# Loading each filler unit's weights one unit sooner in the attention stages of a hybrid attention block

## The chip, the cores and the metric

The kernel runs on one core of a Trainium2 chip. The metric is the device time of one execution, in microseconds (us); lower is better. The engines are named as in the profile: PE is TensorE (matmul), PEld its weight loads, DVE is VectorE, ACT is ScalarE, POOL is GpSimd, and SP is SyncE, whose queue issues most of the DMA transfers.

## The reference

One layer of a streaming encoder, for 1024 positions of 1024 channels, in float32: two attention branches side by side, merged by gates, and a feed-forward part.

```python
h = rms_norm(x, norm_mix[layer])
proj = h @ w_in[layer]
(sb_q, sb_k, sb_v, g_q, g_k, g_v, g_out, g_low, gate_sb, gate_gla) = jnp.split(
    proj, split_points, axis=-1)

o_sb = stick_breaking_attention(split_heads(sb_q, SB_HEADS).astype(f32),
                                split_heads(sb_k, SB_HEADS).astype(f32),
                                split_heads(sb_v, SB_HEADS).astype(f32))
...
o_gla = gla_chunked(split_heads(g_q, GLA_HEADS).astype(f32),
                    split_heads(g_k, GLA_HEADS).astype(f32),
                    split_heads(g_v, GLA_HEADS).astype(f32),
                    split_heads(log_a, GLA_HEADS))
...
mix = (jax.nn.sigmoid(gate_sb) * (o_sb @ w_proj_sb[layer])
       + jax.nn.sigmoid(gate_gla) * (o_gla @ w_proj_gla[layer]))
x = x + mix @ w_out[layer]

h2 = rms_norm(x, norm_mlp[layer])
x = x + jnp.square(jax.nn.relu(h2 @ w_ff1[layer])) @ w_ff2[layer]
return rms_norm(x, norm_final)
```

The stick-breaking attention has 8 heads of 64 channels. For each query it takes the sigmoids of the scores (`beta`) and of their negatives (`fail`), runs a product of the `fail` values over the keys from the nearest back, and weighs the values by `beta` times that product.

## The kernel before

**Products in three parts.** Every float32 operand is split into a high part `hi` (a cast on ACT) and a low part `lo` (a subtraction on DVE), and `mm3` forms hi·hi + hi·lo + lo·hi: three matmuls (lines 115 to 117) for each block of 128 channels.

**Stages.** First the RMSNorm, then the gated linear attention (GLA) of 4 heads, whose result goes to DRAM as `o_gla`, then the stick-breaking attention in four pairs of heads (`sb_core`, p = 0 to 3), then the projection of its result (`pa`), `w_out`, and the feed-forward part. An attention pair has 8 steps (`sb_step`); a step makes scores on PE (`pz`), sigmoids on ACT (`beta`, `fail`, lines 582 and 583), masks on POOL, a running product (line 589, "scan") and a multiplication on DVE, transposes on PE (`ptw`), a split into `w_hi` and `w_lo`, the products with the values (`poa`), and an addition into `o_sb` (line 619).

**Fillers.** Between the steps, `fill(n)` runs n entries of the list `fillers`, projections that don't depend on the step at hand. An entry is half of a unit. A unit has one weight tile of 128x8x128 (512 KB) and two products, one for each half of the positions. `load_cols` (through `load_w`) loads the tile into a buffer `raw` and splits it into `whi` and `wlo`. The pool gives `raw` two buffers (`bufs=2`), and `whi` and `wlo` two each. `queue_gate` units make the gates (`mmt`, then a copy and a store to DRAM). `queue_b` units make `o_gla @ w_proj_gla` (`pb`, line 669), multiply by the sigmoid of a gate (line 673: this also frees the bank of `pb`) and store the result. Fillers accumulate in the two banks of `ps_fill`.

**The last pair.** For p = 3 the list holds the rest of the earlier fillers, the last two gate units with their halves interleaved, and then the 8 `queue_b` units, two and two: first halves of units 0 and 1, then their second halves, and so on. The first `queue_b` entry of each half calls `load_b(half)`: four transfers of o_gla pieces of 512 KB (line 658), each into a `raw` buffer of the same two, each split into a part of `bt_hi` and `bt_lo`. Half 0 and half 1 have tiles of their own.

**What sets the order.** The program is not run in the order in which it is written. A scheduler decides at build time, engine by engine, in which order the instructions stand; each engine, and SP's queue, then takes its instructions strictly in that order, and waits for semaphores where data or a buffer is not ready. Buffers of one tag go round in the order of their allocation in the program.

Of the kernel before, what the change touches and what calls it, by code (L numbers as in the profile page):

```python
# [47 lines left out]
def hybrid_block_kernel(ctx, tc, x, norm_mix, w_in, w_gate_up, b_gate_up, gla_norm, w_proj_sb, w_proj_gla,  # L48
# [114 lines left out]
    stage = ctx.enter_context(tc.tile_pool(name="stage", bufs=2))  # L163

    fillers = []

    def fill(n=1):
        for _ in range(min(n, len(fillers))):
            fillers.pop(0)()

    def queue_unit(load, halves):
        w = []

        def half_unit(i):
            if not w:
                w.append(load())
            halves(w[0], i)

        for i in range(2):
            fillers.append(lambda i=i: half_unit(i))  # L180

    def queue_gate(c0, dst):
        def halves(w, half):
            acc = proj_t(w, half)
            raw = stage.tile([P, HALF], F32, tag="gate", name="gate", bufs=2)
            nc.scalar.copy(out=raw, in_=acc)
            nc.sync.dma_start(out=dst[:, half * HALF:(half + 1) * HALF], in_=raw)

        queue_unit(lambda: load_cols(w_in, c0), halves)
# [97 lines left out]
    def queue_gla_qk(h):  # L287
        res = [[None, None], [None, None]]

        def q_half(w, half):  # L290
            q1 = gw.tile([P, 4, 192], F32, tag="q1", name="q1", bufs=2)
            acc = proj_t(w, half)
            nc.scalar.mul(out=q1[:, :, 64:192], in_=acc.rearrange("p (c t) -> p c t", t=P), mul=float(P) ** -0.5)
            res[half][0] = q1

        def k_half(w, half):
            kT = gw.tile([P, 4, P], F32, tag="kT", name="kT", bufs=2)
            acc = proj_t(w, half)
            nc.scalar.copy(out=flat(kT), in_=acc)
            res[half][1] = kT  # L300

        n = len(fillers)
        queue_unit(lambda: load_cols(w_in, GQ + h * P), q_half)
        queue_unit(lambda: load_cols(w_in, GK + h * P), k_half)
        fillers[n:n + 4] = [fillers[n + i] for i in (0, 2, 1, 3)]
        return res
# [154 lines left out]
    qk = queue_gla_qk(0)  # L461
    vgs = [gla_vg(c, vo) for c in range(VG_START)]
    fill(2)
    for half in range(2):
        sl = slice(half * HALF, (half + 1) * HALF)
# [11 lines left out]

    pre = gla_pre(0, 0, *qk[0])
    fill(2)
    n_gate = 0  # L480
    n_vg = VG_START
    for h in range(G_HEADS):
        nxt = None
        if h + 1 < G_HEADS:
            nxt = queue_gla_qk(h + 1)
        while len(fillers) < sum(GLA_FILL):
            queue_gate(*gates[n_gate])
            n_gate += 1
        pre1 = None
        for c in range(NT):  # L490
            gla_core(h, c, pre if c < 4 else pre1, vgs.pop(0))
            while n_vg < min(h * NT + c + 1 + VG_AHEAD, G_HEADS * NT):
                if n_vg % NT == 0:
                    vo = [load_vo(n_vg // NT, j) for j in range(4)]
                vgs.append(gla_vg(n_vg % NT, vo))
                n_vg += 1
            fill(GLA_FILL[c])
            if c == 1:
                pre1 = gla_pre(h, 1, *qk[1])
            if c == 5 and nxt:  # L500
                pre_n = gla_pre(h + 1, 0, *nxt[0])
        if nxt:
            qk, pre = nxt, pre_n
# [684 lines left out]
```

## Time and profile before

| | us |
|---|---|
| median of 3 runs | 1673.47 |
| lowest and highest run | 1673.26 and 1673.96 |
| the profiled execution, its own time | 1675.34 |
| span of the profile, first to last instruction | 1673.6 |
| PE busy in the span | 1644.1 (98%) |

The mean granted clock of PE was 0.996 of full speed. Times in the trace count from the span's start. The profiled execution is a single one, so a sum made from its rows is compared with its own time first.

### The profile page before, as it was taken

What the parts mean: (1) busy time and instruction counts of PE and PEld (TensorE: products, weight loads), DVE (VectorE), ACT (ScalarE), POOL (GpSimd) and SP (SyncE); (2) the same over time, 40 slices, a digit from 0 to 9 for tenths busy, and PEclk for the clock granted to TensorE, in tenths of its full rate; (3) what the DMA queues carried; (4) which work ended last, traced back from release to release, by engine and by line L of the source; (5) the groups of instructions that cost most, each with busy time, mean ns of one, the idle gap of its engine ahead of it and who ended that gap; (6) DMA issues with size and microseconds to landing.
All of it is one profiled execution on the core that took longest, in us unless ns stands there. A gap on an engine that the chain in (4) does not pass through costs nothing.

```text
span 1673.6 us, 22678 instructions
## 1 busy us (share of the span) xinstructions
PE 1644.1 (98%) x8160; PEld 1377.9 (82%) x8160; DVE 1143.6 (68%) x1954; ACT 762.2 (46%) x1544; POOL 381.1 (23%) x376
## 2 busy tenths in 40 slices
PE   7999999999999999999999999999999999999997
PEld 5788888888888888888888788888888888888886
DVE  7677677665732768677876645887776764787795
ACT  6456455554532656565644422422222234444464
POOL 4001000000010021201110000598777640000161
PEclk9999999999999999999999999999999999999999
DMA  7103104022121121114426643454444467655453
GB/s 215 28 20 108 33 20 126 18 76 66 54 66 39 45 70 27 32 30 148 132 95 201 199 160 101 137 184 159 153 150 156 144 205 236 201 189 171 157 166 123
DMA packets 153952, 194.06 MB, mean 116 GB/s; under 512 B 11712, under 2 KB 91584, under 8 KB 153840
## 3 DMA queue, kind: packets, MB, share of 16 engines
q1 hardware_dynamic: 150464, 189.83, 35.6%
q10 hardware_dynamic: 3376, 2.79, 0.5%
q8 instruction: 64, 1.05, 0.3%
q14 instruction: 48, 0.39, 0.1%
HBM read 138.05 MB, written 54.53 MB: 115 GB/s over the span
## 4 chain that ended last, share of the span: by engine, by line
PE 87%; DMA 5%; DVE 4%; ACT 2%; issue 1%; POOL 1%; SPq 0%; ACTq 0%; POOLq 0%; DVEq 0%
PE mmt L115 7%; PE mmt L117 7%; PE mmt L116 7%; PE pp L115 6%; PE pp L116 6%; PE pp L117 6%; PE pq L117 6%; PE pq L115 6%; PE pq L116 6%; PE mmn L116 4%; PE mmn L117 4%; PE mmn L115 4%; PE sc L408 2%; PE pw L115 2%; PE pw L117 2%; PE pw L116 2%
## 5 line engine op out<-in xcount | busy, mean ns | idle before, releaser
L117 PE MATMUL mmt<-ht_hi,wlo 128*128 128x512 f32 x512 | 201.7, 394 | 2.7 <-DVE wlo L79 2.7
L115 PE MATMUL mmt<-ht_hi,whi 128*128 128x512 f32 x512 | 201.8, 394 | 1.3 <-DVE qs L543 1.3
L116 PE MATMUL mmt<-ht_lo,whi 128*128 128x512 f32 x512 | 201.3, 393 | 0.0
L108 POOL TENSOR_TENSOR rstd<-ms,mhalf 128x1 f32<-128x1 f32 x56 | 41.8, 749 | 648.1 <-DVE ms L104 420.2
L116 PE MATMUL pp<-wlo,whi 128*128 128x512 f32 x448 | 174.4, 389 | 0.0
L117 PE MATMUL pp<-whi,wlo 128*128 128x512 f32 x448 | 174.3, 389 | 0.0
L115 PE MATMUL pp<-whi 128*128 128x512 f32 x448 | 165.8, 389 | 0.0
L79 DVE TENSOR_TENSOR wlo<-raw,whi 128x1024 fp32r<-128x1024 f32 (+1 forms) x110 | 121.2, 1102 | 43.9 <-ACT whi L76 43.5
L76 ACT CAST whi<-raw 128x1024 fp32r<-128x1024 f32 (+1 forms) x112 | 95.8, 866 | 113.9 <-PE pq L116 34.9
L115 PE MATMUL mmn<-whi,ht_hi 128*128 128x512 f32 (+1 forms) x384 | 139.9, 365 | 0.4 <-DVE kl L558 0.4
L116 PE MATMUL mmn<-wlo,ht_hi 128*128 128x512 f32 (+1 forms) x384 | 139.2, 363 | 0.9 <-POOL wlo L79 0.9
L117 PE MATMUL mmn<-whi,ht_lo 128*128 128x512 f32 (+1 forms) x384 | 139.0, 362 | 0.0
L749 DVE TENSOR_TENSOR wlo<-raw,whi 128x512 fp32r<-128x512 f32 (+1 forms) x112 | 89.7, 801 | 68.2 <-ACT whi L1048 49.5
L115 PE MATMUL pq<-s_hi,whi 128*128 128x512 f32 x320 | 126.2, 395 | 0.0
L117 PE MATMUL pq<-s_hi,wlo 128*128 128x512 f32 x320 | 126.0, 394 | 0.0
L116 PE MATMUL pq<-s_lo,whi 128*128 128x512 f32 x320 | 125.6, 393 | 0.0
L1048 ACT CAST whi<-raw 128x512 fp32r<-128x512 f32 x96 | 59.7, 622 | 134.8 <-PE pp L117 68.2
L117 PEld LDWEIGHTS mmt<-ht_hi,wlo 128*128 128x128 f32 x512 | 96.3, 188 | 22.4 <-DVE wlo L79 3.8
L115 PEld LDWEIGHTS mmt<-ht_hi,whi 128*128 128x128 f32 x512 | 96.3, 188 | 19.9 <-issue 1.7
L116 PEld LDWEIGHTS mmt<-ht_lo,whi 128*128 128x128 f32 x512 | 96.4, 188 | 18.5
L115 PEld LDWEIGHTS pp<-whi 128*128 128x128 f32 x448 | 84.1, 188 | 17.6
L117 PEld LDWEIGHTS pp<-whi,wlo 128*128 128x128 f32 x448 | 84.1, 188 | 17.4
(295 smaller groups left out, 4019.0 us busy)
## 6 DMA issues: line engine op xcount, KB each, us to landing
raw<-in_w_in_dram SPq DMA_DIRECT2D x36, 512.0 KB, 4.0
raw<-in_w_ff_dram SPq DMA_DIRECT2D x36, 512.0 KB, 4.4
raw<-aop_S SPq DMA_DIRECT2D x64, 256.0 KB, 2.8
aop_A<-c SPq DMA_DIRECT2D x48, 256.0 KB, 3.2
aop_S<-s SPq DMA_DIRECT2D x48, 256.0 KB, 2.2
raw<-aop_A SPq DMA_DIRECT2D x48, 256.0 KB, 2.7
r<-in_w_ff_dram SPq DMA_DIRECT2D x48, 256.0 KB, 3.1
raw<-in_w_in_dram SPq DMA_DIRECT2D x32, 256.0 KB, 3.2
```

The source lines that it names most:

```text
L76: nc.scalar.copy(out=hi, in_=src)
L79: lo_eng.tensor_tensor(out=lo, in0=src, in1=hi.bitcast(F32), op=ALU.subtract)
L108: rstd_ins.append(nc.gpsimd.tensor_tensor(out=r, in0=ms, in1=mhalf, op=ALU.pow).ins)
L115: nc.tensor.matmul(ps, lhsT=sh, rhs=mh, start=first, stop=False)
L116: nc.tensor.matmul(ps, lhsT=sh, rhs=ml, start=False, stop=False)
L117: nc.tensor.matmul(ps, lhsT=sl, rhs=mh, start=False, stop=last)
L408: nc.tensor.matmul(sc[:P - H, i * 64:(i + 1) * 64], lhsT=lev[H][:, j, :P - H], rhs=right, start=True, stop=True)
L749: eng.tensor_tensor(out=out, in0=in0, in1=in1, op=ALU.subtract)
L1048: nc.scalar.copy(out=hi[:, 0], in_=raw[:, 0])
```

## The change

`queue_unit` registers each unit's load under its two entries (`get`, which does nothing once the tile is loaded). `fill`, before it runs an entry, calls the load of that entry and then the load of the entry that comes next. So in the program a unit's `raw`, `whi` and `wlo` tiles are allocated and its transfer issued one entry sooner, ahead of everything that the entry before allocates and issues. Nothing else is changed; the number of instructions of each kind is the same.

```diff
@@ -163,21 +163,31 @@
     stage = ctx.enter_context(tc.tile_pool(name="stage", bufs=2))
 
     fillers = []
+    loads = {}
 
     def fill(n=1):
         for _ in range(min(n, len(fillers))):
-            fillers.pop(0)()
+            f = fillers.pop(0)
+            if fillers and f in loads:
+                loads.pop(f)()
+            if fillers and fillers[0] in loads:
+                loads.pop(fillers[0])()
+            f()
 
     def queue_unit(load, halves):
         w = []
 
-        def half_unit(i):
+        def get():
             if not w:
                 w.append(load())
+
+        def half_unit(i):
+            get()
             halves(w[0], i)
 
         for i in range(2):
             fillers.append(lambda i=i: half_unit(i))
+            loads[fillers[-1]] = get
 
     def queue_gate(c0, dst):
         def halves(w, half):
```

The order of the instructions, as the scheduler left it, differs from before only in the last attention pair. In what follows, line numbers of the changed kernel are 10 higher than before (L668 is L658 of before, and so on).

**SP's queue, the loads of the last pair.** `raw<-in_w_in_dram` is the weight of a gate unit, `raw<-in_w_proj_gla_dram` that of a `queue_b` unit, `raw<-o_gla` a piece of `load_b`; `gate_a` is a store of a gate, `sg<-gate_b` a load of one. Before:

```order
L85 DMA raw<-in_w_in_dram 128x8x128
L85 DMA raw<-in_w_proj_gla_dram 128x8x128
L187 DMA gate_a<-gate 128x512
L658 DMA raw<-o_gla 128x2x512
L187 DMA gate_a<-gate 128x512 x2
L658 DMA raw<-o_gla 128x2x512 x2
L187 DMA gate_a<-gate 128x512
L658 DMA raw<-o_gla 128x2x512
L85 DMA raw<-in_w_proj_gla_dram 128x8x128
L667 DMA sg<-gate_b 128x512
L187 DMA gate_a<-gate 128x512
L658 DMA raw<-o_gla 128x2x512
```

Now:

```order
L85 DMA raw<-in_w_in_dram 128x8x128
L85 DMA raw<-in_w_proj_gla_dram 128x8x128
L197 DMA gate_a<-gate 128x512
L85 DMA raw<-in_w_proj_gla_dram 128x8x128
L197 DMA gate_a<-gate 128x512 x3
L668 DMA raw<-o_gla 128x2x512
L677 DMA sg<-gate_b 128x512
L197 DMA gate_a<-gate 128x512
L668 DMA raw<-o_gla 128x2x512
L677 DMA sg<-gate_b 128x512
L668 DMA raw<-o_gla 128x2x512 x6
```

The second weight of w_proj_gla stood behind the first four o_gla pieces; it now stands ahead of all eight, which follow in one sequence with no weight between them.

**ACT, where the second half of o_gla is cast.** `bt_hi_8561` is the tile of half 1 (L76 casts a piece of it), `beta` and `fail` are the sigmoids of an attention step. Before:

```order
L76 CAST bt_hi_8561<-raw 128x1024
L604 CAST w_hi<-ptw 128x256
L604 CAST w_hi<-ptw 128x128
L76 CAST bt_hi_8561<-raw 128x1024
L604 CAST w_hi<-ptw 128x128
L668 ACTIVATE sg<-sg 128x512
L582 ACTIVATE beta<-pz 128x512
L583 ACTIVATE fail<-pz 128x512
L582 ACTIVATE beta<-pz 128x384
L583 ACTIVATE fail<-pz 128x384
```

Now:

```order
L76 CAST bt_hi_8561<-raw 128x1024
L614 CAST w_hi<-ptw 128x128
L76 CAST bt_hi_8561<-raw 128x1024
L592 ACTIVATE beta<-pz 128x512
L593 ACTIVATE fail<-pz 128x512
L592 ACTIVATE beta<-pz 128x384
L593 ACTIVATE fail<-pz 128x384
L628 COPY o_sb_5041<-poa 64x256
L614 CAST w_hi<-ptw 128x256
L76 CAST bt_hi_8561<-raw 128x1024
```

The rows ahead of the first fence hold the casts of the first two pieces of half 1. So the four sigmoids stood behind the casts of all four pieces, and now stand behind those of the first two; the casts of the last two pieces moved behind them.

**DVE, at the same place.** `bt_lo_8562` is the low part of half 1, `sg<-pb` (L673, now L683) frees a bank of `pb`. Before:

```order
L79 TENSOR_TENSOR bt_lo_8562<-raw,bt_hi_8561 128x1024
L605 TENSOR_TENSOR w_lo<-ptw,w_hi 128x128
L673 TENSOR_TENSOR sg<-pb,sg 128x512
L589 SCALAR_TENSOR_TENSOR fail<-fail 128x895
L619 TENSOR_TENSOR o_sb_5041<-poa,o_sb_5041 64x256
L591 TENSOR_TENSOR beta<-beta,fail 128x895
L605 TENSOR_TENSOR w_lo<-ptw,w_hi 128x256
```

Now:

```order
L79 TENSOR_TENSOR bt_lo_8562<-raw,bt_hi_8561 128x1024
L615 TENSOR_TENSOR w_lo<-ptw,w_hi 128x128
L79 TENSOR_TENSOR bt_lo_8562<-raw,bt_hi_8561 128x1024
L599 SCALAR_TENSOR_TENSOR fail<-fail 128x895
L629 TENSOR_TENSOR o_sb_5041<-poa,o_sb_5041 64x256
L683 TENSOR_TENSOR sg<-pb,sg 128x512
L615 TENSOR_TENSOR w_lo<-ptw,w_hi 128x256
L601 TENSOR_TENSOR beta<-beta,fail 128x895
L79 TENSOR_TENSOR bt_lo_8562<-raw,bt_hi_8561 128x1024
```

The first release of a `pb` bank stood ahead of the scan of 895 elements; it now stands behind it and behind the addition into `o_sb`, and only the subtractions of the first two pieces of half 1 come ahead of the scan.

## Rows read from the trace of the kernel before

**Rows 1.** Page, parts 1 and 2: busy time and its tenths.
```profile
PE 1644.1 (98%) x8160; PEld 1377.9 (82%) x8160; DVE 1143.6 (68%) x1954; ACT 762.2 (46%) x1544; POOL 381.1 (23%) x376
PE   7999999999999999999999999999999999999997
```

**Rows 2.** Page, part 4: the chain that ended last.
```profile
PE 87%; DMA 5%; DVE 4%; ACT 2%; issue 1%; POOL 1%; SPq 0%; ACTq 0%; POOLq 0%; DVEq 0%
```

**Rows 3.** Two of PE's waits, whole span: us in total, times, longest us.
```profile
PE mmt L117 <- DVE wlo L79: 2.7, 2, 2.2
PE poa L615 <- DVE w_lo L605: 1.9, 1, 1.9
```

**Rows 4.** Waits of PE between 760 and 1010, all there are.
```profile
PE pa L115 <- ACT whi L76: 1.9, 3, 1.0
PE pa L115 <- DVE ma L724: 0.2, 1, 0.2
```

**Rows 5.** Windows of the last attention pair, columns as first row names.
```profile
core 0: us, PE busy (x) PEld busy (x) DVE busy (x) ACT busy (x) POOL busy (x), PEclk, DMA share, GB/s
780.00:790.00 10.00, 10.00 (x59) 8.67 (x58) 7.90 (x14) 7.12 (x14) 1.19 (x4) 1.00 0.67 221
790.00:800.00 10.00, 10.00 (x53) 8.39 (x53) 7.01 (x14) 6.65 (x15) 1.57 (x4) 1.00 0.73 222
```

**Rows 6.** Timeline of SP's queue: loads of the last pair.
```profile
780.42 0.37 SPq L85 DMA_DIRECT2D raw<-in_w_proj_gla_dram  x1
```

**Rows 7.** Line 658, the o_gla loads between 765 and 805: landing times.
```profile
DMA to landing us min/median/max: 3.8/4.2/5.4
```

**Rows 8.** Tile bt_hi: duration in ns, first and last start.
```profile
L76 ACT CAST bt_hi<-raw x8: 1049/1050/1052, 764.8 to 797.5; 128x1024 fp32r<-128x1024 f32 x8
L79 DVE TENSOR_TENSOR bt_lo<-raw,bt_hi x8: 1219/1226/1227, 765.9 to 798.6; 128x1024 fp32r<-128x1024 f32 x8
```

**Rows 9.** Timeline of ACT: start us, us.
```profile
772.19 1.05 ACT L76 CAST whi<-raw 128x1024 fp32r<-128x1024 f32 x1 [0.17 <-PE mmt L116]
...
797.53 1.05 ACT L76 CAST bt_hi<-raw 128x1024 fp32r<-128x1024 f32 x1 [1.61 <-DMA raw<-o_gla]
...
799.18 0.59 ACT L582 ACTIVATE beta<-pz 128x512 f32<-128x512 f32 x1
...
800.50 0.51 ACT L583 ACTIVATE fail<-pz 128x384 f32<-128x384 f32 x1
```

**Rows 10.** Timeline of DVE at the same place.
```profile
799.96 0.68 DVE L673 TENSOR_TENSOR sg<-pb,sg 128x512 f32<-128x512 f32 x1
801.45 2.02 DVE L589 TENSOR_TENSOR_SCAN fail<-fail 128x895 f32<-128x895 f32 x1 [0.81 <-POOL fail L587]
803.51 0.43 DVE L619 TENSOR_TENSOR o_sb<-poa,o_sb 64x256 f32<-64x256 f32 x1
```

**Rows 11.** Timeline of PE: four matmuls of the last pair.
```profile
766.62 0.40 PE L115 MATMUL mmt<-ht_hi,whi 128*128 128x512 f32 x1
...
779.55 0.39 PE L117 MATMUL mmt<-ht_hi,wlo 128*128 128x512 f32 x1
...
780.13 0.40 PE L115 MATMUL pb<-bt_hi,whi 128*128 128x512 f32 x1
...
795.10 0.40 PE L115 MATMUL pb<-bt_hi,whi 128*128 128x512 f32 x1
```

**Rows 12.** A wait of PE, and windows around it and another.
```profile
688.31 0.58 PE L615 MATMUL poa<-w_lo,v 128*128 128x256 f32 x1 [1.94 <-DVE w_lo L605]
...
686.00:688.00 2.00, 0.38 (x2) 0.23 (x2) 1.81 (x3) 0.27 (x1) 1.37 (x2) 0.89 0.00 0
692.00:694.00 2.00, 2.00 (x12) 2.00 (x10) 1.72 (x5) 0.00 (x0) 0.23 (x1) 0.50 0.00 0
694.00:696.00 2.00, 2.00 (x18) 2.00 (x18) 0.47 (x1) 0.90 (x2) 0.00 (x0) 0.91 0.00 0
723.00:727.00 4.00, 1.82 (x8) 1.36 (x8) 3.90 (x6) 2.99 (x6) 0.96 (x2) 1.00 0.07 7
```

## The prediction

> **What bounds the kernel now.** I read the page first: PE (TensorE) is busy 98% of the span and 9 tenths of nearly every slice [rows 1], and the chain that ended last lies 87% on PE [rows 2]. So time is lost only where PE stands still or runs at its lower clock, and the list of PE's waits says where. Behind the start there is little: 2.7 us for a low weight half (`mmt` for `wlo`, two waits, the longest 2.2) and 1.9 us for `poa` [rows 3]. The 2.7 us is what an earlier load seems to be for. Then I asked the same list for the stretch 760 to 1010 alone, where the change moves instructions: no `pb` product waits at all, only `pa`, 1.9 + 0.2 = 2.1 us [rows 4], and PE is busy 10.00 of 10.00 us in 780:790 and in 790:800 [rows 5]. Nothing is to be won in that stretch before the `pa` products, but something can be lost.
>
> **What the change does to the order.** The order on PE, DVE, ACT and SP is that of before, but for shifted line numbers, down to the last attention pair, and POOL's does not change at all. The waits of [rows 3] lie ahead of that point: saved there, 0 us. In the last pair the root is on SP, as the first piece of order shows. Before, the loads into the two `raw` buffers go w_proj_gla(0), four of o_gla, w_proj_gla(1), four of o_gla. Now they go w_proj_gla(0), w_proj_gla(1), eight of o_gla. The number of transfers, casts and subtractions is the same; only the places differ.
>
> **Why the new place costs.** A `raw` buffer comes free when both halves are split off it, and w_proj_gla(1) can be split only when the second `whi` buffer is free, that is, behind the last `mmt` of the last gate unit. Before, one `raw` buffer was held by such a weight for the first gate unit (its cast came at 772.19, 0.17 us behind an `mmt` [rows 9]) while the other carried o_gla; w_proj_gla(1) was only issued at 780.42 [rows 6]. Now both buffers are held by weights, and no o_gla piece can be issued until one is split. The last `mmt` of the gates starts at 779.55 and takes 0.39 us [rows 11]; it ends about 779.95, and its place hardly moves.
>
> Each trip of one o_gla piece is DMA, cast, subtraction: 4.2 us median from issue to landing (3.8 to 5.4) [rows 7], 1.05 us on ACT and 1.23 us on DVE [rows 8], together 6.48 us, after which the next but one piece may be issued. The Trainium skill, "DMA: Bandwidth & Descriptors", section "Anatomy of one DMA — SWDGE (gpsimd) path", gives about 2.0 us + bytes / 436e3 for a transfer of that other path, an estimate of 3.2 us for these 512 KB; the trace has 4.2, and with 3.2 the chain below would be 3.0 us shorter. The second buffer's chain, from 779.95:
> - cast and subtraction of w_proj_gla(1), 1.05 + 1.23 (durations of the same shape [rows 8]): 782.23
> - second o_gla piece of the first half, 6.48: 788.71
> - fourth piece, 6.48: 795.19
> - second piece of the second half, DMA and cast only, 4.2 + 1.05: 800.44
>
> **Who is queued behind it.** ACT takes its instructions in order. The second piece of order shows that the sigmoids of the next attention step (`beta` and `fail` of 512 and of 384) now stand directly behind that cast. Before, they stood behind all four casts of the second half, but the last of those ran at 797.53 [rows 9], so nothing waited long; now they stand behind two, and the second isn't done before 800.4. The four sigmoids take 799.18 to 801.01 = 1.83 us [rows 9]: 802.27. POOL's mask lies between their end and the scan, 801.45 − 801.01 = 0.44: 802.71. On DVE, in order too, the scan of 895 elements (2.02), the `o_sb` addition (0.43) and only then the drain of the first `pb` bank (0.68) follow, as the third piece of order shows [rows 10]; before, the drain stood ahead of the scan. Sum 3.13: 805.84. PE's first product of the second half, `pb` on `bt_hi` half 1, needs that bank, since the ring of filler banks has two and the second product fills the other. A dozen hand-overs between engines lie on this chain; the one in [rows 9] shows 0.17 us. I take 0.45 for all: about **806.3**.
>
> When would PE be there without waits? Before, from the common 766.62 to its first product of the second half at 795.10 [rows 11], PE ran 151 matmuls with 60,160 columns (counted in the order), in 28.48 us without idle. The new order has 17 more ahead of that product, pulled forward from behind it: 4 `pz` of 512, 2 of 384, 4 `poa` of 256, 4 of 128, 3 `ptw`: 4,736 columns, at the same rate 2.24 us. So 797.3. **First term: 806.3 − 797.3 = +9.0 us.** Part of it shows earlier: the first o_gla piece can be issued only when w_proj_gla(0) is split, which I put near 779.2 because its split now stands behind the attention work on ACT and DVE; with 6.48 us it is ready near 785.8. PE started `pb` at 780.13 before [rows 11], and now runs out of other work near 782: a first stop of about 3.7 us, some 2 us of small waits, then a stop of about 3 us that ends at 806.3. These are inside the 9.0. A clock drop behind the first stop is inside it too, since the chain of transfers, not PE, sets 806.3.
>
> **Second term, the clock.** One stop of the trace is like these: PE stood 1.94 us up to 688.31 for `w_lo`; the granted clock began to fall there (0.89 over 686:688), was 0.50, the lower of the two levels (1.2 GHz against 2.4), and came back within 694:696, whose 0.91 puts it at 694.4 [rows 12]. Work at half clock from 688.3 to 694.4 loses half of 6.1 us, 3.1 us. Against it, 2.18 us of idle in 723:727 left the clock at 1.00 [rows 12]. So a stop may cost 0 or 3.1 us. The last stop here is longer than both and follows a thin stretch; I take +3.1.
>
> **Given back.** If PE is 12 us later, the `pa` loads have more time: at most the 2.1 us of [rows 4]. But those waits are for splits whose buffers PE's own progress frees, so they should move along with it: 0 taken. Behind about 820 I found no place in the new order where an engine waits longer than before.
>
> Sum against the profiled execution's own time: 1675.34 + 9.0 + 3.1 = 1687.4. That execution is 1.87 us above the median of the runs; against the median, 1673.47 + 12.1 = **1685.6**. Bounds: with DMA legs of 3.8 us and no drop, 9.0 − 1.2 − 0.45 = +7.3; with one leg of 5.4 and a drop, +13.3.
>
> **Rivals.**
> - *Nothing is lost (0 us).* The late pieces would be hidden by attention work and by the two interleaved `pb` units, each of which uses the same o_gla. For it: no `pb` waits today [rows 4]. Against it: the pieces are 9 to 13 us later, and PE's lead over them is less. It decides itself at the first piece: ready before about 782, nothing is lost. In a sentence aside, the Trainium skill, "Trainium Kernel Development and Optimization", section "Best Practices", advises to double-buffer so that DMA overlaps compute; by it the earlier weight load would cost nothing. The trace bears this out for weights alone; here the same two buffers also feed o_gla.
> - *Only the first stop counts (+4 to +6 us).* If transfers are nearer 3.8 us than 4.2, or the drain isn't held as long as I walked it, PE loses the first stop and a little more: 3.7 to about 6. About 1678.5: 1673.47 + 5.
> - *The stops, without a drop of the clock (+9.0).* 1682.5. The 723:727 row speaks for it, the 688 row against it.
> - *Faster.* It would take the `pa` waits, −2.1 us: 1671.4. That is 0.13% and lies within 0.2% (3.35 us, about what a measurement of this kernel can tell from no change). More would need the drop at 688 to go away, which lies ahead of anything that the change moves.
>
> **How the numbers follow.** Both stops with the drop, about +12: 0.40. Without the drop, +7 to +10: 0.27. First stop only, +4 to +6: 0.13. Worse than +15 (two drops that count, or a further wait behind 806): 0.05. No change: 0.12. Faster by over 0.2%: 0.03. So faster 0.03, within 0.2% 0.12, slower 0.85. The likeliest case gives the time, 1685.6. From the first-stop case (1677.5) to the likeliest with a slow transfer (1673.47 + 13.3 = 1686.8) and some of the worse, 1677 to 1689 leaves out about 0.18.
>
> **What would show it.** In the changed profile: the waits on `mmt` and `poa` of [rows 3] unchanged ahead of 760; w_proj_gla(1) issued ahead of every o_gla piece, and the first o_gla only near 779; the o_gla pieces about 6.5 us apart in each buffer; new PE waits between 781 and 807 of about 9 us in all; a granted clock near 0.5 for some 6 us behind 806; the `pa` waits still there. If `pb` runs without waits from 780 on, or the clock stays at 1.00 behind the stops, the first or the second term is wrong. If that piece is issued before 776, my reading of who holds the `raw` buffers is wrong.

## The result and the profile after

The changed kernel takes 1693.03 us (median; 1692.61 to 1693.98, 4 runs) against 1673.72 us for the kernel before in the same series: 1.0114 times, 95% interval 1.0099 to 1.0130. It is 19.3 us slower. The forecast was 12.1 us slower and a range up to 1689; the direction was right and the size too small. The profiled execution of after has a span of 1691.1 us, 17.5 us more than that of before; that of before lay 1.6 us above the median of its own series, so the sums below are made between the two spans.

The page of after, its busy line:

```profile
PE 1651.4 (98%) x8160; PEld 1379.2 (82%) x8160; DVE 1142.8 (68%) x1954; ACT 762.0 (45%) x1544; POOL 376.8 (22%) x376
```

PE is as busy as before in share. In the chain that ended last, `DMA mix_b<-sg`, the store of a `pb` product, stood three times before, with 7.5 us in all; now it stands there seven times, with 29.8 us, or 2% of the span. Nothing in the prediction spoke of it.

The three largest groups of PE's waits of after between 760 and 1020 (us in total, times, longest), which answer to [rows 4]:

```profile
PE pa L115 <- ACT whi L76: 3.6, 4, 1.2
PE poa L623 <- ACT w_hi L614: 2.3, 3, 1.3
PE poa L623 <- DVE o_sb L629: 2.3, 1, 2.3
```

Where only `pa` waited, attention products now wait for ACT and for `o_sb`, and `pa` itself waits 3.6 us instead of 1.9. The waits ahead of 760 are those of [rows 3] to the tenth of a us.

Matmuls of PE in after: the first `pb`, the first `pb` of the second half, the first `pa`, the first `pw` behind the `pa` products.

```profile
784.45 0.50 PE L115 MATMUL pb<-bt_hi,whi 128*128 128x512 f32 x1 [0.58 <-ACT bt_hi L76]
...
805.62 0.50 PE L115 MATMUL pb<-bt_hi,whi 128*128 128x512 f32 x1 [0.28 <-DVE sg L683]
...
915.05 0.47 PE L115 MATMUL pa<-oa_hi,whi 128*128 128x512 f32 x1 [0.61 <-ACT whi L76]
...
964.88 0.40 PE L115 MATMUL pw<-wo_hi,mixt_hi 128*128 128x512 f32 x1
```

The first two answer to 780.13 and 795.10 of [rows 11]. Of before, the last two:

```profile
899.71 0.39 PE L115 MATMUL pa<-oa_hi,whi 128*128 128x512 f32 x1
...
947.11 0.40 PE L115 MATMUL pw<-wo_hi,mixt_hi 128*128 128x512 f32 x1
```

So PE is 805.62 − 795.10 = 10.5 us later at the second half of `pb`, of which 2.2 us is work pulled forward (8.3 us lost), 915.05 − 899.71 = 15.3 us at the first `pa`, and 964.88 − 947.11 = 17.8 us at the first `pw`; from there to the end it stays, within 0.3 us. The loss has three parts: 8.3 up to 806, 7.0 from there to `pa`, 2.4 in `pa`. I had foreseen the first and a part of the second.

Windows of after, columns as in [rows 5]:

```profile
780.00:790.00 10.00, 8.06 (x33) 5.87 (x32) 6.97 (x11) 6.95 (x14) 1.49 (x4) 0.83 0.73 234
800.00:805.00 5.00, 2.73 (x14) 1.87 (x12) 3.80 (x4) 4.07 (x9) 0.58 (x2) 1.00 0.68 202
805.00:810.00 5.00, 4.72 (x14) 3.63 (x15) 5.00 (x7) 3.29 (x6) 1.17 (x1) 0.70 0.19 64
810.00:815.00 5.00, 5.00 (x24) 4.18 (x24) 3.80 (x4) 0.63 (x2) 0.48 (x2) 0.96 0.62 192
820.00:840.00 20.00, 17.59 (x89) 13.53 (x88) 13.53 (x17) 9.53 (x20) 1.12 (x4) 1.00 0.40 119
840.00:860.00 20.00, 18.74 (x105) 16.00 (x104) 13.74 (x17) 10.01 (x23) 2.39 (x6) 1.00 0.27 92
920.00:940.00 20.00, 18.21 (x79) 14.17 (x77) 15.78 (x23) 8.94 (x15) 0.00 (x0) 1.00 0.75 234
940.00:960.00 20.00, 17.95 (x76) 13.50 (x74) 15.09 (x24) 9.57 (x16) 0.00 (x0) 1.00 0.73 234
```

PE stands for 1.9 us in 780:790 and 2.3 us in 800:805, its granted clock is 0.83, then 0.70 and 0.96; it stands again for 2.4 + 1.3 us in 820:860, and for 1.8 + 2.0 us in 920:960. Before, the same windows read:

```profile
820.00:840.00 20.00, 20.00 (x112) 17.33 (x111) 15.91 (x21) 10.54 (x25) 1.66 (x6) 1.00 0.28 93
920.00:940.00 20.00, 18.45 (x79) 14.09 (x78) 13.89 (x22) 10.25 (x18) 0.00 (x0) 1.00 0.75 249
940.00:960.00 20.00, 19.29 (x81) 14.58 (x80) 13.72 (x20) 8.27 (x13) 0.00 (x0) 1.00 0.44 141
```

Before, 820:840 has no idle time, and 920:960 has 2.3 us.

### The profile page after: what moved, and what is told of

Same layout as the page of the kernel before. It is cut to its first block, busy times and chain, and to the rows that moved or that the text cites. A ratio compares the mean times of both kernels' runs of the same rounds, so it can differ in the third digit from the quotient of the medians.

```text
span 1691.1 us, 22676 instructions
## 1 busy us (share of the span) xinstructions
PE 1651.4 (98%) x8160; PEld 1379.2 (82%) x8160; DVE 1142.8 (68%) x1954; ACT 762.0 (45%) x1544; POOL 376.8 (22%) x376
## 4 chain that ended last, share of the span: by engine, by line
PE 87%; DMA 6%; DVE 4%; ACT 2%; issue 1%; POOL 0%; SPq 0%; ACTq 0%; DVEq 0%; POOLq 0%
PE mmt L117 7%; PE mmt L115 7%; PE mmt L116 7%; PE pp L115 6%; PE pp L117 6%; PE pp L116 6%; PE pq L115 6%; PE pq L117 6%; PE pq L116 6%; PE mmn L115 4%; PE mmn L117 4%; PE mmn L116 4%; DMA mix_b<-sg 2%; PE sc L418 2%; PE pw L115 2%; PE pw L117 2%
## 5 line engine op out<-in xcount | busy, mean ns | idle before, releaser
L76 ACT CAST whi<-raw 128x1024 fp32r<-128x1024 f32 (+1 forms) x112 | 96.0, 867 | 114.7 <-PE pq L116 36.8
L116 PEld LDWEIGHTS pp<-wlo,whi 128*128 128x128 f32 x448 | 84.1, 188 | 17.6
L117 PEld LDWEIGHTS pp<-whi,wlo 128*128 128x128 f32 x448 | 84.1, 188 | 17.5
```

Of the source, the lines that this page charges most:

```text
L76: nc.scalar.copy(out=hi, in_=src)
L116: nc.tensor.matmul(ps, lhsT=sh, rhs=ml, start=False, stop=False)
L117: nc.tensor.matmul(ps, lhsT=sl, rhs=mh, start=False, stop=last)
```

## The experiments

Each kernel was timed against the kernel before on the same chip, so the ratio is what to read. Where one gives a tile another buffer, the scheduler makes an order of its own around it.

**Without the one load (unit1_late).** Among SP's loads the two orders part at the place of one weight, so I left that one load as it was before.

```diff
...
-        queue_unit(lambda: load_cols(w_proj_gla, ct * P), halves)
+        queue_unit(lambda: load_cols(w_proj_gla, ct * P), halves, early=ct != 1)
```

> The change for every unit but w_proj_gla(1), which is loaded when its own entry runs, as before. All five engines then have the order of before, word for word. Theory (the whole loss comes from this one load): 1673.5 us, no new PE wait between 760 and 900. Rival (earlier program order of the other loads costs or wins something by itself): anything else, above all around the gate and q/k units; 2 us or more off.

1673.42 us, ratio 1.0002 (0.9992 to 1.0011). On every engine the order is that of before. So the whole of the loss comes from loading w_proj_gla(1) sooner, together with the order that the scheduler then makes; all the other units loaded sooner, in the attention pairs too, change neither the order nor the time.

**The early weight in a buffer of its own (raw1_own).** The last pair has no next pair, so the second `qs0` buffer is unused.

```diff
...
+            raw = sp.tile([P, T], F32R, tag="qs0", name="raw1", bufs=2).bitcast(F32).rearrange("p (k c) -> p k c", k=KT)
+            nc.sync.dma_start(out=raw, in_=w_proj_gla[:, P:2 * P].rearrange("(k p) c -> p k c", p=P))
...
```

> The change whole, but the raw piece of w_proj_gla(1) goes into a buffer that the last attention pair leaves unused, not into the two raw buffers; its split still waits for the second whi buffer. Theory (the early weight costs because it holds a raw buffer that o_gla needs): the o_gla pieces are issued near 767, 774 and 782 as before, PE runs 780:806 without a stop, and the time is 1672 to 1677. Rival (the early load costs by its place in the queues, whoever holds the buffer): 1685 or more.

1674.64 us, ratio 1.0006 (0.9996 to 1.0015). SP's queue, where line 668 loads o_gla and line 690 the early weight:

```profile
751.82 0.37 SPq L668 DMA_DIRECT2D raw<-o_gla  x1
...
772.93 6.25 SPq L668 DMA_DIRECT2D raw<-o_gla  x2
779.27 0.42 SPq L690 DMA_DIRECT2D raw<-in_w_proj_gla_dram  x1
```

The first o_gla piece goes at 751.8 and the fourth and fifth from 772.9 on, all ahead of the weight (before, four were ahead of it). In the changed kernel the first goes at 779.24:

```profile
753.40 0.37 SPq L85 DMA_DIRECT2D raw<-in_w_proj_gla_dram  x1
...
779.24 0.37 SPq L668 DMA_DIRECT2D raw<-o_gla  x1
...
782.43 0.37 SPq L668 DMA_DIRECT2D raw<-o_gla  x1
```

The row at 753.40 is the early weight. The piece at 779.24 goes as soon as w_proj_gla(0) is split (the subtraction ends at 779.21), and the piece at 782.43 as soon as the early weight is split (its cast begins at 780.10, see below; the subtraction ends at 782.41). These two rows show the hold of both buffers. The run raw1_own shows less: with a buffer of its own the scheduler puts the weight at 779.27, so nothing is loaded early there, and the time is back with the old place of the o_gla loads. That a weight landed at 753 in a buffer of its own would cost nothing isn't shown.

**More buffers for the gates (gate_ring).** This asks for the loss behind 806. A `pb` product is multiplied by a gate in `sg`; `sg` has two buffers, and each is loaded again only when the product in it is stored.

```diff
...
-            sg = stage.tile([P, HALF], F32, tag="gate", name="sg", bufs=2)
+            n_sg[0] += 1
+            if 2 < n_sg[0] <= 6:
+                if not sgs:
+                    sgs.extend(sp.tile([P, T], F32R, tag=f"kl{e}", name="sg", bufs=2) for e in range(2))
+                i = n_sg[0] - 3
+                sg = sgs[i // 2].bitcast(F32)[:, i % 2 * HALF:(i % 2 + 1) * HALF]
+            else:
+                sg = stage.tile([P, HALF], F32, tag="gate", name="sg", bufs=2)
```

> The change whole, and the third to sixth gate loads of w_proj_gla units (sg) get four buffers of their own. Theory (what I did not foresee, some 4.5 us between 820 and 850 and 2.4 us in pa, is the gate ring: its first release stands behind the scan, so every later gate load and its sigmoid, queued ahead of the w_hi casts on ACT, comes late): the waits of 781:806 stay near 8 to 10 us, those of 820:850 go, the time is 1685 to 1689. Rival (the interleaving of attention and pb in the new order, not late gates): 1691 to 1695.

1682.03 us, ratio 1.0052 (1.0037 to 1.0067): 11 us less than the change, 3 us below the range that I gave. Its windows:

```profile
820.00:840.00 20.00, 20.00 (x106) 16.92 (x105) 14.24 (x19) 7.79 (x18) 1.13 (x4) 1.00 0.30 97
840.00:860.00 20.00, 20.00 (x115) 17.43 (x114) 15.50 (x20) 10.98 (x24) 3.13 (x8) 1.00 0.29 92
920.00:940.00 20.00, 20.00 (x88) 16.15 (x87) 16.55 (x26) 10.10 (x16) 0.00 (x0) 1.00 0.76 249
940.00:960.00 20.00, 19.31 (x83) 15.16 (x82) 14.81 (x24) 9.28 (x16) 0.00 (x0) 1.00 0.64 213
```

PE doesn't stand at all between 820 and 860, and in 920:960 it stands 0.7 us. The stop that I had predicted is still there: `poa` waits 2.3 us for `o_sb`, as in the change. PE's order in gate_ring is another than in the change from 785.9 on, so this run alone doesn't part late gates from the interleaving. The rows of after in the next section do that for the stops of 820:860: at the two longest the gate is named. Of the 10.8 us between the two spans, 5.4 come between the first `pb` and the first `pa`, and 5.7 in `pa`, which takes 44.2 us to the first `pw` here, 49.8 in the change and 47.4 before. It is shorter here than before, so for `pa` the order counts too, and the gates are only the likely cause.

**The same gate buffers in the kernel before (gate_ring_before).** The edit is the same.

> The kernel before with the same four gate buffers, as the control. Theory: PE did not wait in 780:900 before, so 0 there; at most the 2.1 us of pa waits go: 1671.3 to 1674. Rival (gate buffers are worth something by themselves): 1670 or less.

1679.65 us, ratio 1.0039 (1.0026 to 1.0052): slower, which neither side had. PE's waits between 740 and 1000:

```profile
PE pa L115 <- ACT whi L76: 2.7, 4, 1.2
PE pb L117 <- DVE wlo L79: 2.0, 1, 2.0
```

A `pb` now waits 2.0 us for a low weight half, and `pa` waits longer than before: the scheduler, given free gate buffers, found another order of loads in SP's queue. So the price of a gate buffer by itself can't be read from either run, and how the 11 us above divide between gates that come sooner and an order that happens to be better stays open; only the stops of 820:860 are placed.

**Four buffers for o_gla (ogla_ring).** The pieces take the unused buffers of `qs` and `ks`.

```diff
...
-            raw = wp.tile([P, 2, HALF], F32, tag="raw", name="raw", bufs=2)
+            if k // 2 >= len(spare):
+                spare.append(sp.tile([P, T], F32R, tag=("qs0", "qs1", "ks0", "ks1")[k // 2], name="spare", bufs=2))
+            raw = spare[k // 2].bitcast(F32).rearrange("p (k t) -> p k t", k=2)
```

> The change whole, but the o_gla pieces get four buffers of their own, so that no weight holds one of theirs. In SP's order the load of w_proj_gla(2) now stands ahead of the first o_gla piece, and it waits for the raw buffer of w_proj_gla(0). Theory (a piece is late if the queue ahead of it or its buffer waits for a weight's split): the first piece is still issued near 779 and the first stop of some 4 us at 782:786 stays; the pieces then come two and two, the stop at 803:806 and the waits of 820:850 go: 1676 to 1680. Rival (buffers alone decide): 1672 to 1675 without any stop. Rival (neither; the order itself costs): 1690 or more.

1683.97 us, ratio 1.0061 (1.0046 to 1.0076), some 4 us above my forecast. The place was right: SP issues the first piece, whose buffer is free, only behind the load of w_proj_gla(2), which waits until w_proj_gla(0) is split (777.55):

```profile
777.57 0.38 SPq L85 DMA_DIRECT2D raw<-in_w_proj_gla_dram  x1
778.06 1.04 SPq L671 DMA_DIRECT2D spare<-o_gla  x2
```

All but 0.3 us of the waits of 820:850 are gone. But four pieces, two weights and gates now travel at once, and a piece takes

```profile
DMA to landing us min/median/max: 3.9/7.0/9.8
```

where the pieces of the changed kernel took

```profile
DMA to landing us min/median/max: 3.7/3.9/4.5
```

PE stands in two of the windows behind it:

```profile
780.00:784.00 4.00, 1.90 (x7) 1.12 (x7) 3.81 (x8) 2.63 (x8) 1.49 (x4) 1.00 1.01 306
792.00:796.00 4.00, 2.23 (x8) 1.27 (x8) 2.92 (x4) 3.95 (x10) 0.58 (x2) 1.00 0.72 244
```

More buffers moved the stop at 803 ahead of 800, and PE stands for 5.7 us in 780:810, against 4.5 in the change. Over all runs, what goes with the loss is the time of the first o_gla piece: where it goes at 778 to 779 (the change, gate_ring, ogla_ring) the kernel is 8.5 us or more behind, whether a held buffer or a load ahead of it in SP's queue delays the piece. Where it goes at 751 to 753 the time is that of before, but for gate_ring_before, with its wait of a `pb` for `wlo`.

**Both (raw1_own_gate_ring).** The edits of raw1_own and gate_ring in one kernel.

> The early weight in a buffer of its own, and the four gate buffers besides. Theory: neither the hold nor the gate ring costs any more, and as in the change with gate buffers the pa waits (2 to 2.5 us) go: 1670 to 1672.5. Rival (as with the kernel before and gate buffers, the order that the scheduler finds costs more than the buffers bring): 1674 to 1680.

1673.54 us, ratio 1.0000 (0.9990 to 1.0009): between the two expectations, back at before, and without the gain in `pa` that I had hoped for; PE still waits 1.6 us for `pa` weights there.

**What the waits ahead of 760 are (qk_low_on_pool).** The change looks made for the 2.2 us that an `mmt` waits for `wlo` [rows 3]. Before, SP issued the last two weights ahead of that wait at 699.9 to 702.9, ACT cast `whi` when an `mmt` freed its buffer, and DVE subtracted behind an attention multiplication:

```profile
723.33 1.09 DVE L591 TENSOR_TENSOR beta<-beta,fail 128x895 f32<-128x895 f32 x1
724.34 1.22 DVE L79 TENSOR_TENSOR wlo<-raw,whi 128x1024 fp32r<-128x1024 f32 x1
```

```profile
720.98 1.05 ACT L76 CAST whi<-raw 128x1024 fp32r<-128x1024 f32 x1 [0.15 <-PE mmt L116]
```

```profile
699.92 2.98 SPq L85 DMA_DIRECT2D raw<-in_w_in_dram  x2
```

The transfer had been over for some 14 us (the later of the two was issued at 702.53 and took 4.2 us to land). To take DVE's queue out of it, I gave the low halves of the q and k weights to POOL in pairs 1 to 3.

```diff
...
-        queue_unit(lambda: load_cols(w_in, SBQ + p * P), q_half)
-        queue_unit(lambda: load_cols(w_in, SBK + p * P), k_half)
+        queue_unit(lambda: load_cols(w_in, SBQ + p * P, lo_eng=nc.gpsimd if p else nc.vector), q_half)
+        queue_unit(lambda: load_cols(w_in, SBK + p * P, lo_eng=nc.gpsimd if p else nc.vector), k_half)
```

> The kernel before, with the low halves of the q and k weights of pairs 1 to 3 subtracted on POOL (2.4 to 2.9 us each there) and not on DVE (1.23). It asks what the waits are that the change left in place (mmt for wlo 2.2 us at 723). Theory (the transfer had landed long before; the split waits for the whi buffer and then in DVE's queue behind a scan): the wait at 723 shrinks to about 1.5 us or less, 1671 to 1674. Rival (the load itself was late): the wait stays 2.2 us or grows by POOL's slower subtraction, 1673.5 to 1677.

1684.82 us, ratio 1.0066 (1.0051 to 1.0081): slower, as neither side had it. The wait for `wlo` did shrink, from 2.7 to 0.5 us in all, but at 721 a `poa` now waits 4.7 us for `w_lo`. Why stands in the last section; that stop and the lower clock behind it are not all of the 11.5 us, and `pa` waits 2.6 us more as well. So the run is no clean test of the split's place; that the load wasn't late rests on the rows above.

**The same step in pa (pa_weights_sooner).** In the kernel before, `pa` waits for weights. There each weight is loaded one product pair sooner.

```diff
...
-            whi, wlo = load_cols(w_proj_sb, ct * P, nk=4)
+            whi, wlo = nxt
+            if ct + 1 < KT:
+                nxt = load_cols(w_proj_sb, (ct + 1) * P, nk=4)
```

> The kernel before, with each w_proj_sb weight of the pa products loaded one product pair sooner, the same step as the change, but in the stage where PE does wait for such a weight (1.9 us). Theory (an earlier load helps where the wait is for the load and hurts where it takes a buffer that another load needs; here the w_out pieces share the two raw buffers): the 1.9 us go or turn into waits for w_out, 1671.5 to 1674. Rival (sooner is always safe): exactly 1.9 us less, 1671.6, and no new wait.

1672.09 us, ratio 0.9991 (0.9982 to 1.0001). PE's waits between 740 and 1000, all there are:

```profile
PE pw L115 <- DVE ma L727: 1.6, 1, 1.6
PE pa L117 <- DVE wlo L79: 0.5, 1, 0.5
```

The 1.9 us of `pa` are gone, and `pw` waits 1.6 us for the last `ma` in their place. Of a repeat with more runs I expected:

> The kernel before with the pa weights one product pair sooner, in more rounds, to tell its 1.2 us from nothing. If the gain is real the ratio is 0.9985 to 0.9995 with an interval that ends below 1; if not, the interval holds 1.

1673.44 us, ratio 0.9995 (0.9987 to 1.0004): the interval holds 1, so no gain can be claimed.

**All three together (all_three)**, the two buffers and the sooner `pa` weights:

> The change whole, with the raw piece of w_proj_gla(1) in a buffer of its own, four gate buffers, and the w_proj_sb weights of pa one product pair sooner. Theory: the first two bring the kernel back to before, the third alone wins what it won there (1672.09 against 1673.34): 1671.5 to 1672.7, ratio 0.999. Rival (the order that the scheduler finds around pa shifts again): 1673 to 1676.

1673.83 us, ratio 1.0003 (0.9994 to 1.0012), on the rival's side. No version here is shown to beat the kernel before.

## Why the prediction was too small

**The place and the cause were right.** The order differed only in the last pair, the waits ahead of it stayed, and the one load that moved past the o_gla pieces made the loss (unit1_late). The chain that I walked came out nearly to the us. ACT in after:

```profile
780.10 1.05 ACT L76 CAST whi<-raw 128x1024 fp32r<-128x1024 f32 x1 [3.46 <-PE mmt L116]
...
799.13 1.05 ACT L76 CAST bt_hi<-raw 128x1024 fp32r<-128x1024 f32 x1 [1.29 <-DMA raw<-o_gla]
```

DVE in after:

```profile
802.36 2.02 DVE L599 TENSOR_TENSOR_SCAN fail<-fail 128x895 f32<-128x895 f32 x1 [0.93 <-POOL fail L597]
804.87 0.69 DVE L683 TENSOR_TENSOR sg<-pb,sg 128x512 f32<-128x512 f32 x1
```

The weight was cast at 780.10 (forecast 779.95), the second piece of the second half at 799.13 to 800.18 (800.44), the sigmoids ended at 801.92 (802.27), the drain began at 804.87 and PE went on at 805.62 (806.3). **First term: 8.3 us measured, 9.0 forecast.** The two full trips came out as forecast, 13.0 us together; the last piece landed 0.5 us sooner than the 4.2 of [rows 7], and the hand-overs took less than the 0.45 that I allowed. What ended most of the stop I had one instruction off: PE stood 2.27 us at a `poa` for the `o_sb` addition, which is just ahead of the drain on DVE, and only 0.28 us for the bank itself. And PE did not stand for 9 us up to there, but for 4.5; the rest of the delay is the clock and stretches thin in matmuls (33 in 780:790, where before had 59 [rows 5]). The first product started at 784.45, not near 785.8, since it needs the cast and not yet the subtraction. One thing that I wrote of the kernel before was wrong without harm to the sum: the `raw` buffers do not go round in the order of allocation. Before, the o_gla pieces at 767.18 and 773.3 each went right behind the split of the piece ahead of them (767.16 and 773.29), so through one and the same buffer, while the weight held the other.

**Second term, the clock: 1.7 us measured, 3.1 forecast.** Behind the stop at 803 the granted clock was 0.70 over 805:810 and 0.96 over 810:815, so 0.30 × 5 + 0.04 × 5 = 1.7 us. A drop behind the first stop was there too (0.83 over 780:790, 1.7 us), and was absorbed, as I had argued, since the 805.62 is set by the transfers. I took the longest drop of the trace for the price of this stop.

**The step that failed** is this: "Behind about 820 I found no place in the new order where an engine waits longer than before." 7.0 us were lost between 806 and the first `pa`, of which the clock is 1.7; PE's idle time accounts for 3.7 in 820:860 and 0.6 in 900:920, and 1.0 I can't put on a row. For 820:860 it is the gate ring. I had seen that the first drain of a `pb` bank would stand behind the scan, and counted what PE waits for the bank. The same drain also lets the product be stored, and only the store lets the next gate be loaded. The drains came at 804.87 and 808.28 instead of 789.81 and, by [rows 10], 799.96: 15 and 8 us late, where PE itself was 10.5 us late. The gate's sigmoid stands in ACT's queue, and behind it the `w_hi` casts that PE needs. SP's queue and ACT at that place in after:

```profile
825.58 0.32 SPq L684 DMA_DIRECT2D mix_b<-sg  x1
829.87 0.32 SPq L677 DMA_DIRECT2D sg<-gate_b  x1
```

```profile
833.05 0.63 ACT L678 ACTIVATE sg<-sg 128x512 f32<-128x512 f32 x1 [4.74 <-DMA sg<-gate_b]
833.58 0.57 ACT L614 CAST w_hi<-ptw 128x512 fp32r<-128x512 f32 x1
```

The store goes at 825.58, the next load at 829.87, and ACT waits 4.74 us for it; the `w_hi` cast right behind it is what a `poa` waits for at 834.20 (0.76 us). At 842.97 ACT has waited 5.41 us for the next gate, and the `w_hi` cast that follows at 845.00 is what a `poa` waits for at 845.63 (1.26 us). The gate_ring kernel, whose only edit is to this ring, has none of these stops.

The drains are not the whole of it. The stores from the first drain to 862 also took longer to land than before. In after, then before:

```profile
DMA to landing us min/median/max: 2.0/3.8/5.7
DMA to landing us min/median/max: 2.0/2.0/4.6
```

A gate's load goes only when the store has landed, as at 829.87, so a late landing is passed on too. The weights of w_proj_gla(2) to (5) now travel in this stretch, issued at 810.41 to 830.28 and before at 796.77 to 817.78; that they slow the stores is not shown.

ACT waited for gates before too, 27.3 us in all between 760 and 1000 against 43.0 now, so the ring was the next thing to be short.

**"Given back: 0"** had the wrong sign. `pa` lost 2.4 us more, a size known to about 1.4 us, since in unit1_late, with the order of before, the same stretch took 46.0 us and not 47.4. The last gate load goes at 910.96 in SP's queue, and a w_out piece stands behind it and a store: it goes at 915.66 instead of 896.51, 19.2 us later, where PE is 15.3 us later. That this is the cause is argued, not shown.

**The sum.** 8.3 + 1.7 + 5.3 + 2.4 = 17.7, and the spans differ by 17.5. Of these, 7.7 us weren't in the forecast, and of the 12.1 us that I forecast 2.1 were too much; the two misses partly cancel. The rivals with a smaller loss were wrong; "a further wait behind 806", which I gave 0.05, is what happened.

## What to carry to other kernels

A load that is issued sooner takes its buffer sooner: look not at whether the transfer is hidden, but at who else lives in that ring of buffers and how long the early tile must hold its place until it can be used up. When a stop is found in an order, follow every release that hangs on the late instruction to its end (here a bank, but also a store, a gate's buffer and a sigmoid in ACT's queue), and not only the one that the bottleneck waits for. And before moving a load, read when it lands and what its consumer waits for: the 2.2 us that invited this change were a wait for a `whi` buffer and a place in DVE's queue, with the data there for some 14 us.

## What the hardware showed beyond that

**The same stop, another clock.** Up to the last pair all kernels here but qk_low_on_pool have one order. PE stands for 1.9 to 2.1 us at 686 to 688 in each. In the profile of before the granted clock was then 0.50 for some 6 us [rows 12]; in that of gate_ring_before it stayed at 1.00:

```profile
686.00:688.00 2.00, 0.26 (x2) 0.12 (x1) 1.81 (x3) 0.16 (x1) 1.25 (x2) 1.00 0.00 0
692.00:694.00 2.00, 2.00 (x20) 2.00 (x19) 1.97 (x6) 1.33 (x3) 0.00 (x0) 1.00 0.00 0
```

So one stop costs 0 or 3 us in one and the same order of instructions, and by the other profiles values between. Runs of the kernel before spread from 1671.6 to 1676.6 us; whether these drops make that spread I haven't shown.

**Two engines, one interface.** In qk_low_on_pool DVE's multiplication of `beta` by `fail`, 128x895, took 3.05 us where it takes 1.09 elsewhere, and POOL's subtraction, 2.4 us in most places, took 3.59. DVE and POOL there:

```profile
621.99 2.88 DVE L589 TENSOR_TENSOR_SCAN fail<-fail 128x255 f32<-128x255 f32 x1
...
721.16 3.05 DVE L591 TENSOR_TENSOR beta<-beta,fail 128x895 f32<-128x895 f32 x1
```

```profile
719.68 3.59 POOL L79 TENSOR_TENSOR wlo<-raw,whi 128x1024 fp32r<-128x1024 f32 x1 [0.60 <-ACT whi L76]
```

POOL was done at 723.27 and DVE at 724.21, 0.94 us later, nearly as if the multiplication had begun when the subtraction ended. The scan at 621.99, both of whose inputs are `fail`, ran beside another of these subtractions (621.81 to 624.33) and took 2.88 us, where a scan of 255 elements takes 0.68. Beside the other four, DVE ran only instructions with one input from a product's bank, such as `o_sb<-poa,o_sb`, and each took its usual time. The Trainium skill, "Advanced Engine Details and Errata", section "GPSIMD Details", says that the Pool engine shares a read and a write interface with DVE, in conflict with DVE instructions that have two SBUF inputs. The multiplication and the scan have two, and the trace agrees.
